# The last row of a down projection, multiplied in two parts of the tokens

## The chip, the cores and the metric

The kernel runs on one core of a Trainium2 chip. The metric is the device time of one execution in microseconds (us). A core has TensorE (PE in the rows; its weight loads are shown as PEld), VectorE (DVE), ScalarE (ACT), GpSimd (POOL) and the queues that issue transfers (SPq and ACTq are those of SyncE and ScalarE).

## What is computed

One layer of a hybrid decoder for 288 tokens (256 of a prompt and 8 x 4 new ones), model width 1024. The part that matters is the end, the feed-forward block:

```python
h = rmsnorm(x, n_mlp_pre)
f = jnp.square(jax.nn.relu(h @ w_up)) @ w_down      # 1024 -> 4096 -> 1024
x = x + rmsnorm(f, n_mlp_post)
```

The root mean square of `f` is taken over all 1024 features of a token, so no token's output can be finished before all features of that token are known.

## The kernel before

Activations lie transposed: features on the 128 partitions, tokens along the columns. `x` and `mg` are 128 x 8 x 288 (eight rows of 128 features). Weights come from memory in blocks of two sub-blocks of 128 x 1024; `split_w` (L163, L164) splits each into a high and a low part of the rounded type fp32r, on ScalarE and VectorE. `take(s)` hands out sub-block s and has the next one split ahead; the parts come from the pool `splp` with three buffers. A second pool, `spx`, with two buffers, is used earlier in the kernel.

`mm3` (L200 to L202) forms one product with three matmuls: high times high, high times low, low times high. Each is a matmul of 288 columns with a weight load of its own.

The down projection (L826 to L833) runs over eight rows `m` of 128 output features; each sums 32 products `kc` (four sub-blocks of eight), so 96 matmuls, in one PSUM tile `dn`. After a row, `post` (L720, L721) takes the square into `q_f` and the row times its gain into `mg` on ScalarE, and VectorE adds the square to `ssf`. The square of row 7 is not added there: it goes to the norm as a second summand.

Behind row 7 the tail is written in a fixed order (`manual_schedule`, L838): `rsqrt_rows` multiplies `ssf` and the last square with a matrix of 1/1024, which sums over partitions (L208, plain fp32, two passes for each matmul in the rows), then the reciprocal root on ScalarE (L212) and a correction in three VectorE steps (L216 to L218) give the scale `s3` of all 288 tokens. Meanwhile TensorE puts `x` for rows 0 to 4 into PSUM through an identity (L841). Then VectorE multiplies rows of `mg` by the scale (L844), TensorE adds them to the sums (L847), ScalarE copies these out (L848); rows 5 and 6 are added by VectorE (L850) and row 7 is scaled and added by GpSimd (L851, L852) from a copy of the scale (L842). Five transfers (L853, L854) bring the eight rows to `o_y`, four from SP's queue and the last, rows 3 and 4, from ScalarE's.

Of the kernel before, what the change touches and what calls it, by code (L numbers as in the profile page):

```python
# [10 lines left out]
F32 = mybir.dt.float32  # L11
# [5 lines left out]
P = 128  # L17
D = 1024
KC = D // P
# [4 lines left out]
NT = SEQ + ND  # L24
# [5 lines left out]
PAST = 1024  # L30
EPS = 1e-6


LAST = ((0, 1), (1, 3), (3, 5), (5, 7))
PE_SUM = 5

POOL_LO = (24, 25)
POOL_ML = (1,)
# [23 lines left out]
V_PRE, V_POST, V_MPRE, V_MPOST, V_ATT, V_CONV, V_TAP = 0, 8, 16, 24, 32, 36, 40  # L62
# [42 lines left out]


@with_exitstack
def layer(ctx, tc, xt, vec, cst, kt, vt, st, wts, o_y, o_k, o_v, o_cs):
    nc = tc.nc
    cp = ctx.enter_context(tc.tile_pool(name="cp", bufs=1))  # L110
    act = ctx.enter_context(tc.tile_pool(name="act", bufs=6))
    nrm = ctx.enter_context(tc.tile_pool(name="nrm", bufs=1))
    rawp = ctx.enter_context(tc.tile_pool(name="rawp", bufs=3))
    splp = ctx.enter_context(tc.tile_pool(name="splp", bufs=3))
    ec = ExitStack()
    cv = ec.enter_context(tc.tile_pool(name="cv", bufs=1))
    pg = ctx.enter_context(tc.tile_pool(name="pg", bufs=2, space=PSUM))
# [9 lines left out]
    x = cp.tile([P, KC, NT], F32, name="x")  # L127
    vv = cp.tile([P, V_END], F32, name="vv")
# [17 lines left out]
    m1024 = cp.tile([P, P], F32, name="m1024")  # L146
    nc.vector.memset(m1024, 1.0 / 1024)
    ident = cp.tile([P, P], F32, name="ident")
# [7 lines left out]
    def split_w(s, parts=1, pool=splp, eng=None):  # L156
        raw = blocks[s // 2][:, (s % 2) * 1024:(s % 2) * 1024 + 1024]
        hi = pool.tile([P, 1024], F32R, tag="hi", name=f"hi{s}")
        lo = pool.tile([P, 1024], F32R, tag="lo", name=f"lo{s}")
        n = 1024 // parts  # L160
        for i in range(parts):
            cs = slice(i * n, (i + 1) * n)
            a = nc.scalar.copy(hi[:, cs], raw[:, cs])  # L163
            b = (eng or nc.vector).tensor_sub(lo[:, cs], raw[:, cs], hi[:, cs].bitcast(F32))  # L164
        splits[s] = a.ins, b.ins
        return hi, lo
# [10 lines left out]
    ready = {}  # L177

    def ahead(s):
        if s < 96 and s not in ready:  # L180
            ready[s] = split_w(s, parts=4 if s in (1, 2) or 25 <= s <= 28 else 1, eng=nc.gpsimd if s in POOL_LO else None)

    def take(s, n=1):

        ahead(s)
        for i in range(1, n + 1):
            ahead(s + i)
        return ready.pop(s)
# [8 lines left out]
    def mm3(ps, w, j, xh, xl, start, stop):  # L197
        hi, lo = w
        a = hi[:, j * P:(j + 1) * P]
        nc.tensor.matmul(ps, lhsT=a, rhs=xh, start=start, stop=False)  # L200
        nc.tensor.matmul(ps, lhsT=a, rhs=xl, start=False, stop=False)  # L201
        return nc.tensor.matmul(ps, lhsT=lo[:, j * P:(j + 1) * P], rhs=xh, start=False, stop=stop)  # L202

    def rsqrt_rows(ssq, mean_w, n, dst, nm, pool=None, tag="g"):

        ps = (pool or pg).tile([P, 512], F32, tag=tag, name=f"ss_{nm}")
        for i, q in enumerate(ssq):
            nc.tensor.matmul(ps[:, :n], lhsT=mean_w, rhs=q, start=i == 0, stop=i == len(ssq) - 1)  # L208
        y = nrm.tile([P, NT], F32, tag="y", name=f"y_{nm}")
        t = nrm.tile([P, NT], F32, tag="t", name=f"t_{nm}")  # L210
        if nm == "f":
            e = nc.scalar.activation(y[:, :n], ps[:, :n], AF.Abs_reciprocal_sqrt, bias=epsc)  # L212
        else:
            nc.scalar.activation(y[:, :n], ps[:, :n], AF.Ln, bias=epsc)
            e = nc.scalar.activation(y[:, :n], y[:, :n], AF.Exp, scale=-0.5)
        nc.vector.scalar_tensor_tensor(t[:, :n], y[:, :n], -0.5, y[:, :n], ALU.mult, ALU.mult)  # L216
        nc.vector.scalar_tensor_tensor(t[:, :n], ps[:, :n], EPS, t[:, :n], ALU.add, ALU.mult)
        d = nc.vector.scalar_tensor_tensor(dst, t[:, :n], 1.5, y[:, :n], ALU.add, ALU.mult)  # L218
        return e.ins, d.ins

    def gemm(ps, w, bh, bl, between=()):

        for kc in range(KC):
            if 0 <= kc - 3 < len(between):
                between[kc - 3]()
            last = mm3(ps[:, :NT], w, kc, bh[kc // 4][:, kc % 4], bl[kc // 4][:, kc % 4], kc == 0, kc == KC - 1)
        return last.ins
# [43 lines left out]
    c = ap.tile([P, C_END], F32, name="c")  # L271
# [71 lines left out]
    with tc.manual_schedule(engines={mybir.EngineType.PE, mybir.EngineType.DVE, mybir.EngineType.Activation}):  # L343
# [4 lines left out]
        for kc in range(3):  # L348
            input_square(kc)
        ahead(4)  # L350
        for kc in range(3, 5):
            input_square(kc)
# [78 lines left out]
    def p_values(p):  # L431
        pts = []
        for j in range(2):
            s = soft.pop((p, j))
            tp = pa.tile([P, 512], F32, tag="a", name=f"tp{p}{j}")
            for i in range(3):
                nc.tensor.transpose(tp[:, i * P:(i + 1) * P], s[:, i * P:(i + 1) * P], ident)
            pt = sm.tile([P, 3 * P], F32, tag="pt", name=f"pt{p}{j}")
            nc.scalar.copy(pt, tp[:, 0:3 * P])
            pts.append(pt)  # L440
        return [lambda: p_sum(p, pts)]
# [188 lines left out]
    p = p_values(0)  # L630
    p_scores(1)
    conv_u(0, 13, p + [lambda: 0, lambda: d_transpose(0)])
    p = p_values(1)
# [6 lines left out]
    p = p_values(2)  # L640
# [6 lines left out]
    p = p_values(3)  # L647
# [21 lines left out]
    pt = ctx.enter_context(tc.tile_pool(name="pt", bufs=6, space=PSUM))  # L669
    spx = ctx.enter_context(tc.tile_pool(name="spx", bufs=2, side="right"))  # L670
# [17 lines left out]
    ws = [take(24, 0)]  # L688
# [20 lines left out]
    tp = ctx.enter_context(tc.tile_pool(name="tp", bufs=1))  # L709
    tw = ctx.enter_context(tc.tile_pool(name="tw", bufs=2))  # L710
    mg = tp.tile([P, KC, NT], F32, name="mg")
    fh = tp.tile([P, 32, NT], F32R, name="fh")
    fl = tp.tile([P, 32, NT], F32R, name="fl")

    def post(ps, m, vcol, dst, ssq, nm):

        t = ssq
        if m:
            t = tw.tile([P, NT], F32, tag="q", name=f"q_{nm}{m}")
        nc.scalar.square(t, ps[:, :NT])  # L720
        nc.scalar.mul(dst, ps[:, :NT], vv[:, vcol + m:vcol + m + 1])  # L721
        if 0 < m < 7:
            nc.vector.tensor_add(ssq, ssq, t)
        return t
# [7 lines left out]
    for m in range(8):  # L732
        if m < NW:
            mix_half(m, 1, False)
            ps = pss[m]
        else:
            w = take(24 + m, m < 7)
            ps = pt.tile([P, 512], F32, tag="o", name=f"mix{m}")
            gemm(ps, w, mh, ml)
        last = post(ps, m, V_POST, mg[:, m], ssm, "m")  # L740
# [4 lines left out]
    hl = [act.tile([P, 4, NT], F32R, tag="act", name=f"hl{i}") for i in range(2)]  # L745

    rsqrt_rows([ssm, last], m1024, NT, s1, "mix")
    warm(WARM1, "mix", last)
    ss1 = tp.tile([P, NT], F32, tag="ss1", name="ss1")
# [35 lines left out]
    ws = [take(32 + m, 0) for m in range(2)] + [split_w(34 + m, pool=spx) for m in range(2)]  # L785
# [25 lines left out]
    for m in range(NW, 32):  # L811
        w = take(32 + m)
        ps = (pg if m == 6 else pt).tile([P, 512], F32, tag="g" if m == 6 else "o", name=f"up{m}")
        last = gemm(ps, w, hh, hl)
# [8 lines left out]
    with tc.issue_after(evacuated):  # L823
        nc.scalar.preload_act_table_set("abs_reciprocal_sqrt_and_small")
    ssf = tp.tile([P, NT], F32, tag="ssm", name="ssf")
    for m in range(8):  # L826
        ps = pt.tile([P, 512], F32, tag="o", name=f"dn{m}")
        for j in range(4):
            w = take(64 + 4 * m + j)
            for k in range(8):  # L830
                kc = 8 * j + k
                mm3(ps[:, :NT], w, k, fh[:, kc], fl[:, kc], kc == 0, kc == 31)
        last = post(ps, m, V_MPOST, mg[:, m], ssf, "f")  # L833

    s3 = pg.tile([P, 512], F32, tag="g", name="s3")[:, :NT]
    s3c = nrm.tile([P, NT], F32, tag="s", name="s3c")
    sums = [pt.tile([P, 512], F32, tag="o", name=f"sum{m}") for m in range(PE_SUM)]
    with tc.manual_schedule(engines={mybir.EngineType.PE, mybir.EngineType.DVE, mybir.EngineType.Activation}):  # L838
        rsqrt_rows([ssf, last], m1024, NT, s3, "f")
        for m in range(PE_SUM):  # L840
            nc.tensor.matmul(sums[m][:, :NT], lhsT=ident, rhs=x[:, m], start=True, stop=False)  # L841
        nc.scalar.copy(s3c, s3)  # L842
        for a, b in LAST:
            nc.vector.tensor_mul(mg[:, a:b], mg[:, a:b], s3.unsqueeze(1).to_broadcast([P, b - a, NT]))  # L844
            if a < PE_SUM:
                for m in range(a, b):
                    nc.tensor.matmul(sums[m][:, :NT], lhsT=ident, rhs=mg[:, m], start=False, stop=True)  # L847
                    nc.scalar.copy(mg[:, m], sums[m][:, :NT])  # L848
            else:
                nc.vector.tensor_add(mg[:, a:b], mg[:, a:b], x[:, a:b])  # L850
    nc.gpsimd.tensor_mul(mg[:, 7], mg[:, 7], s3c)  # L851
    nc.gpsimd.tensor_add(mg[:, 7], mg[:, 7], x[:, 7])  # L852
    for e, a, b in ((nc.sync, 0, 1), (nc.sync, 7, 8), (nc.sync, 1, 3), (nc.sync, 5, 7), (nc.scalar, 3, 5)):  # L853
        e.dma_start(out=o_y[:, a:b], in_=mg[:, a:b])  # L854


# [61 lines left out]
```

## Time and profile before

| | us |
|---|---|
| time, median of 2 runs | 378.39 (378.39 to 378.40) |
| time of the profiled execution | 378.67 |
| its span | 376.9 |
| TensorE busy | 366.9 |
| VectorE busy | 226.6 |
| ScalarE busy | 198.6 |

The rows come from one profiled execution. A row gives engine, line, operation, and the tiles as output <- inputs. A matmul's duration reaches from its start to its modelled end; matmuls overlap, so the distance between starts and the duration differ.

### The profile page before, as it was taken

Reading aid. Unit: us, or ns where it says so; the run is one execution under the profiler, and the core shown is the slowest. Engines: PE = TensorE matmul, PEld = TensorE weight load, DVE = VectorE, ACT = ScalarE, POOL = GpSimd, SP = SyncE. Lnnn points to the kernel's source line nnn. Section 1 sums busy time; section 2 is a strip of 40 time slices with the busy share of each in tenths; the row PEclk is TensorE's granted clock in tenths of the full one; section 3 lists DMA queues with packets and bytes.
Section 4 is the critical chain, followed back from the end, with each engine's and each line's share of the span. In section 5 each row is a group of like instructions: output and inputs, shape, how many; then the busy total and the mean of one; then the engine's idle time right before and its main releaser. Section 6 shows DMA issues by size and latency. Waiting matters only on the chain.

```text
span 376.9 us, 6798 instructions
## 1 busy us (share of the span) xinstructions
PE 366.9 (97%) x2738; PEld 338.6 (90%) x2738; DVE 226.6 (60%) x414; ACT 198.6 (53%) x373; POOL 29.8 (8%) x56
## 2 busy tenths in 40 slices
PE   7999999999999999999999999999999999999994
PEld 6899688676885899899999999999999999999992
DVE  3889766457385877598886666666434344434404
ACT  4879546443463857446775555555533344434412
POOL 0006100114223300000000000000000000000001
PEclk9999999999999999999999999999999999999999
DMA  7995699986993426503435445453535263533003
GB/s 212 420 406 205 246 393 421 407 339 250 405 418 133 129 103 225 222 3 113 178 156 163 174 148 190 138 198 123 213 118 217 111 216 121 202 135 111 2 0 125
DMA packets 17647, 76.23 MB, mean 202 GB/s; under 512 B 2000, under 2 KB 7632, under 8 KB 10704
## 3 DMA queue, kind: packets, MB, share of 16 engines
q1 hardware_dynamic: 16464, 74.26, 52.8%
q10 hardware_dynamic: 1152, 1.54, 1.1%
q8 instruction: 21, 0.34, 0.3%
q14 instruction: 10, 0.08, 0.1%
HBM read 73.40 MB, written 2.40 MB: 201 GB/s over the span
## 4 chain that ended last, share of the span: by engine, by line
PE 86%; DVE 6%; ACT 2%; DMA 2%; issue 1%; SPq 1%; POOL 0%; DVEq 0%; ACTq 0%
PE dn L200 9%; PE dn L202 9%; PE dn L201 9%; PE up L200 8%; PE up L202 8%; PE up L201 8%; PE d L470 3%; PE dpv L514 2%; PE mix L202 2%; PE mix L200 2%; PE mix L201 2%; DMA raw<-wts 2%; PE qk L202 2%; PE qk L200 2%; PE qk L201 2%; PE u L200 1%
## 5 line engine op out<-in xcount | busy, mean ns | idle before, releaser
L164 DVE TENSOR_TENSOR lo<-raw,hi 128x1024 fp32r<-128x1024 f32 (+1 forms) x99 | 112.1, 1140 | 78.6 <-ACT hi L163 78.4
L163 ACT CAST hi<-raw 128x1024 fp32r<-128x1024 f32 (+1 forms) x104 | 97.5, 950 | 96.4 <-PE dn L201 55.3
L200 PE MATMUL dn<-fh,hi 128*128 128x288 f32 x256 | 75.8, 296 | 0.0
L201 PE MATMUL dn<-fl,hi 128*128 128x288 f32 x256 | 75.6, 295 | 0.0
L202 PE MATMUL dn<-fh,lo 128*128 128x288 f32 x256 | 75.3, 294 | 0.0
L201 PE MATMUL up<-hl,hi 128*128 128x288 f32 x248 | 73.4, 296 | 0.0
L200 PE MATMUL up<-hh,hi 128*128 128x288 f32 x248 | 73.1, 296 | 0.0
L202 PE MATMUL up<-hh,lo 128*128 128x288 f32 x248 | 72.9, 294 | 0.0
L202 PEld LDWEIGHTS dn<-fh,lo 128*128 128x128 f32 x256 | 48.2, 188 | 0.0
L201 PEld LDWEIGHTS dn<-fl,hi 128*128 128x128 f32 x256 | 48.0, 188 | 0.0
L200 PEld LDWEIGHTS dn<-fh,hi 128*128 128x128 f32 x256 | 48.0, 187 | 0.0
L202 PEld LDWEIGHTS up<-hh,lo 128*128 128x128 f32 x248 | 46.7, 188 | 0.1
L201 PEld LDWEIGHTS up<-hl,hi 128*128 128x128 f32 x248 | 46.6, 188 | 0.1
L200 PEld LDWEIGHTS up<-hh,hi 128*128 128x128 f32 x248 | 46.4, 187 | 0.0
L795 DVE SCALAR_TENSOR_TENSOR r<-up,s 128x288 f32<-128x288 f32 x32 | 14.2, 456 | 14.1 <-PE up L202 14.1
L200 PE MATMUL mix<-mh,hi 128*128 128x288 f32 x64 | 19.3, 302 | 0.0
L851 POOL TENSOR_TENSOR mg<-mg,s3c 128x288 f32<-128x288 f32 x1 | 0.8, 795 | 233.7 <-ACT s3c L842 233.7
L201 PE MATMUL mix<-ml,hi 128*128 128x288 f32 x64 | 19.0, 296 | 0.0
L202 PE MATMUL mix<-mh,lo 128*128 128x288 f32 x64 | 18.9, 295 | 0.0
L798 DVE TENSOR_TENSOR fl<-r,fh 128x288 fp32r<-128x288 f32 x32 | 14.0, 450 | 0.0
L797 ACT CAST fh<-r 128x288 fp32r<-128x288 f32 x32 | 13.3, 431 | 0.7
L796 ACT ACTIVATE r<-r 128x288 f32<-128x288 f32 x32 | 13.5, 438 | 0.0
(241 smaller groups left out, 637.6 us busy)
## 6 DMA issues: line engine op xcount, KB each, us to landing
raw<-wts SPq DMA_DIRECT2D x45, 1024.0 KB, 4.8
k<-kt SPq DMA_DIRECT2D x16, 640.0 KB, 11.7
v<-vt SPq DMA_DIRECT2D x9, 1024.0 KB, 11.7
raw<-wts SPq DMA_DIRECT2D x4, 512.0 KB, 8.5
v<-vt SPq DMA_DIRECT2D x2, 512.0 KB, 11.0
c<-cst SPq DMA_DIRECT2D x1, 838.0 KB, 9.7
raw<-wts SPq DMA_DIRECT2D x3, 256.0 KB, 5.3
x<-xt SPq DMA_DIRECT2D x4, 144.0 KB, 3.5
```

The source lines that it names most:

```text
L163: a = nc.scalar.copy(hi[:, cs], raw[:, cs])
L164: b = (eng or nc.vector).tensor_sub(lo[:, cs], raw[:, cs], hi[:, cs].bitcast(F32))
L200: nc.tensor.matmul(ps, lhsT=a, rhs=xh, start=start, stop=False)
L201: nc.tensor.matmul(ps, lhsT=a, rhs=xl, start=False, stop=False)
L202: return nc.tensor.matmul(ps, lhsT=lo[:, j * P:(j + 1) * P], rhs=xh, start=False, stop=stop)
L470: nc.tensor.matmul(ps[32 * i:32 * i + 32, 0:n], lhsT=qbd[:, p, 4 * g + i], rhs=t[:, i, 0:n], start=p == 0, stop=p == 3, tile_position=(0, ...
L514: nc.tensor.matmul(dpv[g][32 * i:32 * i + 32], lhsT=pt[:, j, 32 * i:32 * i + 32], rhs=t[i], start=False, stop=j == 4, tile_position=(0, 32 ...
L795: nc.vector.scalar_tensor_tensor(r, ps[:, :NT], 0.0, s2, ALU.max, ALU.mult)
L796: nc.scalar.square(r, r)
L797: a = nc.scalar.copy(fh[:, m], r)
L798: nc.vector.tensor_sub(fl[:, m], r, fh[:, m].bitcast(F32))
L851: nc.gpsimd.tensor_mul(mg[:, 7], mg[:, 7], s3c)
```

## The change

Row 7 leaves the loop. Its products are formed twice: first for tokens 0 to 159 (`last[0]`), then for tokens 160 to 287 (`last[1]`). Six of the 32 steps into the second part (18 matmuls) the norm of the first part is put into TensorE's order, and its scaling and addition run on VectorE. After the second part the same follows for its 128 tokens, with rows 0 to 3 added on TensorE in one matmul of 512 columns and rows 4 to 7 on VectorE. GpSimd no longer takes part. The sub-blocks 92 and 93 are split into the pool `spx`. The output is two tensors, one for each part, written by two transfers each.

```diff
-            ready[s] = split_w(s, parts=4 if s in (1, 2) or 25 <= s <= 28 else 1, eng=nc.gpsimd if s in POOL_LO else None)
+            ready[s] = split_w(s, pool=spx if s in (92, 93) else splp, parts=4 if s in (1, 2) or 25 <= s <= 28 else 1, eng=nc.gpsimd if s in POOL_LO else None)
...
             nc.tensor.matmul(ps[:, :n], lhsT=mean_w, rhs=q, start=i == 0, stop=i == len(ssq) - 1)
+            if mid and i == 0:
+                mid()
...
-    for m in range(8):
+    for m in range(7):
...
+    def last_row(i, kc):
+        if len(ws) <= kc // 8:
+            ws.append(take(92 + kc // 8))
+        c = cols[i]
+        mm3(last[i][:, :c.stop - c.start], ws[kc // 8], kc % 8, fh[:, kc, c], fl[:, kc, c], kc == 0, kc == 31)
...
+    def evac_last(i):
+        n = cols[i].stop - cols[i].start
+        nc.scalar.square(qs[i][:, :n], last[i][:, :n])
+        nc.scalar.mul(mg[:, 7, cols[i]], last[i][:, :n], vv[:, V_MPOST + 7:V_MPOST + 8])
+
+    def scaled(i, h):
+        n = cols[i].stop - cols[i].start
+        a = mg[:, 4 * h:4 * h + 4, cols[i]]
+        nc.vector.tensor_mul(a, a, sc[i][:, :n].unsqueeze(1).to_broadcast([P, 4, n]))
+        return a
+
+    def summed(i, h):
+        nc.vector.tensor_add(ys[i][h], mg[:, 4 * h:4 * h + 4, cols[i]], x[:, 4 * h:4 * h + 4, cols[i]])
+
+    def scales(i, mid=None):
+        n = cols[i].stop - cols[i].start
+        rsqrt_rows([ssf[:, cols[i]], qs[i][:, :n]], m1024, n, sc[i][:, :n], f"f{i}", mid=mid)
+
+    for kc in range(32):
+        last_row(0, kc)
+    evac_last(0)
...
+        for kc in range(6):
+            last_row(1, kc)
+        scales(0)
+        for kc in range(6, 32):
+            last_row(1, kc)
+        for h in range(2):
+            scaled(0, h)
+            summed(0, h)
+        evac_last(1)
+
+        scales(1, lambda: nc.tensor.matmul(xs, lhsT=ident, rhs=x[:, 0:4, cols[1]], start=True, stop=False))
+        nc.tensor.matmul(xs, lhsT=ident, rhs=scaled(1, 0), start=False, stop=True)
+        nc.scalar.copy(ys[1][0].rearrange("p a t -> p (a t)"), xs)
+        scaled(1, 1)
+        summed(1, 1)
+    for h in range(2):
+        nc.sync.dma_start(out=o_ya[:, h], in_=ys[0][h])
+    nc.sync.dma_start(out=o_yb[:, 1], in_=ys[1][1])
+    nc.scalar.dma_start(out=o_yb[:, 0], in_=ys[1][0])
```

## Rows read from the trace of the kernel before

**Rows 1.** The page, busy us, share of the span and instructions of an engine.
```profile
PE 366.9 (97%) x2738; PEld 338.6 (90%) x2738; DVE 226.6 (60%) x414; ACT 198.6 (53%) x373; POOL 29.8 (8%) x56
```
**Rows 2.** The page, chain that ended last, shares of the span by engine.
```profile
PE 86%; DVE 6%; ACT 2%; DMA 2%; issue 1%; SPq 1%; POOL 0%; DVEq 0%; ACTq 0%
```
**Rows 3.** Busy time by stretch: stretch, length, engines, granted clock, DMA share, GB/s.
```profile
165.00:352.00 187.00, 186.75 (x1400) 186.41 (x1399) 107.11 (x148) 95.16 (x148) 0.00 (x0) 1.00 0.43 153
352.00:365.40 13.40, 13.40 (x103) 13.40 (x102) 2.82 (x3) 2.80 (x4) 0.00 (x0) 1.00 0.00 1
365.40:376.90 11.50, 6.69 (x26) 4.12 (x24) 4.59 (x8) 3.69 (x9) 1.59 (x2) 0.98 0.28 103
```
**Rows 4.** Groups by line and shape, TensorE: busy us, mean ns, idle before.
```profile
L200 PE MATMUL dn<-fh,hi 128*128 128x288 f32 x256 | 75.8, 296 | 0.0
```
**Rows 5.** Order of time, 365.4 us to the end: start us, us, what.
```profile
365.40 0.65 PE L208 MATMUL ss_f<-ssf,m 128*128 128x288 f32 x2
365.60 0.41 ACT L720 ACTIVATE q_f<-dn 128x288 f32<-128x288 f32 x1 [8.68 <-PE dn L202]
...
366.06 0.75 PE L208 MATMUL ss_f<-q_f,m 128*128 128x288 f32 x2
...
366.65 2.59 PE L841 MATMUL sum<-x,ident 128*128 128x288 f32 x10
366.85 0.50 ACT L212 ACTIVATE y_f<-ss_f,epsc 128x288 f32<-128x288 f32 x1 [0.45 <-PE ss_f L208]
367.38 0.46 DVE L216 SCALAR_TENSOR_TENSOR t_f<-y_f 128x288 f32<-128x288 f32 x1 [9.21 <-ACT y_f L212]
...
368.37 0.47 DVE L218 SCALAR_TENSOR_TENSOR s<-t_f,y_f 128x288 f32<-128x288 f32 x1
...
369.30 2.45 DVE L844 TENSOR_TENSOR mg<-mg,s 128x288 f32<-128x288 f32 x4 [0.46 <-ACT s3c L842]
...
369.81 2.87 PE L847 MATMUL sum<-mg,ident 128*128 128x288 f32 x10 [0.57 <-DVE mg L844]
...
370.60 0.40 ACT L848 COPY mg<-sum 128x288 f32<-128x288 f32 x1 [1.33 <-PE sum L847]
...
371.78 0.76 DVE L850 TENSOR_TENSOR mg<-mg,x 128x576 f32<-128x576 f32 x1
373.14 0.34 ACTq L854 DMA_DIRECT2D o_y<-mg  x1
```
**Rows 6.** Order of time near 120 us: eight matmuls of 16 columns and their loads.
```profile
120.31 0.99 PEld L525 LDWEIGHTS dsel<-c,om 128*128 128x128 f32 x8
```
**Rows 7.** Order of time and group by shape: warm-up passes of 128 columns.
```profile
155.16 3.29 PE L243 MATMUL warm_mix<-q_m,m 128*128 128x128 f32 x28
...
L243 PE MATMUL warm_mix<-q_m,m 128*128 128x128 f32 x28 | 3.3, 275 | 0.0
```
**Rows 8.** Groups by line and shape, weight loads: busy us, mean ns, idle before.
```profile
L202 PEld LDWEIGHTS dn<-fh,lo 128*128 128x128 f32 x256 | 48.2, 188 | 0.0
...
L470 PEld LDWEIGHTS d<-k,qbd 128*32 128x32 f32 x128 | 3.6, 109 | 4.1 <-issue 1.7 <-POOL k L464 0.3
...
L525 PEld LDWEIGHTS dsel<-c,om 128*128 128x128 f32 x16 | 2.3, 190 | 0.0
```
**Rows 9.** Groups by line and shape, ScalarE: busy us, mean ns, idle before.
```profile
L497 ACT COPY dpt<-dt 128x512 f32<-128x512 f32 x2 | 1.2, 578 | 0.1
...
L214 ACT ACTIVATE y_attd<-ss_attd,epsc 128x32 f32<-128x32 f32 x1 | 0.3, 287 | 0.1
```
**Rows 10.** DMA issues from 340 us on: KB each, median us to landing.
```profile
o_y<-mg SPq DMA_DIRECT2D x2, 288.0 KB, 2.3
o_y<-mg SPq DMA_DIRECT2D x2, 144.0 KB, 1.8
o_y<-mg ACTq DMA_DIRECT2D x1, 288.0 KB, 2.7
```

## What the change was predicted to do

> **What bounds the kernel now.** The page comes first: TensorE is busy for 366.9 of 376.9 us [rows 1], and the chain that ended last runs over TensorE for 86% of the span [rows 2]. The next view is the table of stretches. Between 165 and 352 us, 1400 products take 187.00 us, 0.1336 us each, at the full granted clock (2.4 GHz), and TensorE does not pause. The last 11.5 us hold only 6.69 us of it [rows 3]. So two things set the time: the pitch of the products, and the tail behind the last one.
>
> The pitch first. A product has 288 columns and lasts 296 ns in the row by shape [rows 4], but the next starts after 0.134 us, so the pitch is the price, not the duration. Each product brings a 128x128 weight load of its own: the loads (338.6 us busy) number as many as the matmuls, 2738 [rows 1].
>
> The tail is read from the order of time [rows 5]. The last product's columns are through when the first matmul of ss_f starts at 365.40; I call this T0. The square starts at T0+0.20, ss_f's second pair at T0+0.66, the reciprocal root at T0+1.45, three VectorE steps of about 0.49 each from T0+1.98 on (the third at T0+2.97), the first multiplication at T0+3.90, and from there VectorE, TensorE and ScalarE hand pairs of rows on until the last output transfer is issued at 373.14, T0+7.74. The span ends 3.76 us later, at 376.9.
>
> **The change part by part.**
>
> *The products.* Row 7's 96 products of 288 columns become 96 of 160 and 96 of 128. The columns stay the same, 96 x 288, but the weight loads double: 96 more. What a product costs when its columns no longer cover its load is the term that decides, and no product of the split (fp32r) type with fewer than 288 columns is in the trace. Its neighbours are. In dsel eight matmuls of only 16 columns stand in a row: eight loads in 0.99 us, the last lasting 0.19, so (0.99 - 0.19)/7 = 0.114 us from load to load, though there is next to nothing to stream [rows 6]. In the warm-up, 28 passes of 128 columns take 3.29 us, one lasts 0.275: 3.01/27 = 0.112 us [rows 7]. A load's length grows from 109 ns (32 columns) to 188 (128) [rows 8]: 79 ns for 96 columns, 0.82 ns each, so 128 columns occupy the load path for at least 0.105 us; the rest of the 188 ns is latency that overlaps. Loads of the products' type and of the unsplit type last 188 and 190 ns [rows 8], so I take 0.112 us for each of the 192: 21.5 us in place of 96 x 0.1336 = 12.8. The products get **8.7 us dearer**. Lower bound: 0.105, +7.3 us. Upper bound: the pitch of 0.1336 does not fall at all, because it is already that of the loads and not of the columns: 96 x 0.1336 = +12.8 us.
>
> The Trainium skill (TensorE: Matmul & The Clock Gate, Back-to-back issue gap) gives about 81 ns for a pair of load and matmul at 128 columns; by it 192 would be 15.6 us, an estimate, and the products would get only 2.8 us dearer. The same page's section on LDWEIGHTS gives columns / 1.2, 107 ns for a load, which speaks against this change; the 0.112 to 0.114 us of this trace agree with the second.
>
> *The first part's end.* Square, scaling, ss_f0, root, two multiplications and two additions over 160 tokens run behind the second part. Its cover: after the insertion 26 x 3 products remain, 78 x 0.112 = 8.7 us, against under 6 us of chain: 1.45 + 0.53 + 3 x 0.5 to the scale at most [rows 5], then two pairs of VectorE passes over 640 elements, each about 0.76 + 64 x 1.04 ns = 0.83 us (288 elements take 0.46, 576 take 0.76: 1.04 ns for one [rows 5]), 3.3 us together: 6.8 at the very most. If the cover were gone, that would be added. The 18 products ahead of the insertion (2.0 us) cover the square and its latency of some 0.66. Only ss_f0's four passes of 160 columns stand on TensorE. A pass of 288 takes (2.59 - 0.17)/10 = 0.242 [rows 5] (0.17 is the latency that the 0.275 of a 128-column pass has beyond its pitch of 0.112 [rows 7]), one of 128 0.112, so 0.81 ns a column: 0.138 for 160, **+0.55 us**.
>
> *The weights.* Splits 92 and 93 move to the other pool, so all four stand while both parts use them. Row 7 lasted 12.8 us, and in the 13.40 us up to T0 ScalarE was busy for 2.80 and VectorE for 2.82, with no weight transfer left (1 GB/s) [rows 3]. A group of 24 products lasts 2.7 us now in place of 3.2, so the splits stay hidden; uncovered, one would cost TensorE at most the 2.8 us.
>
> *The tail,* by the same steps with 128 columns. ScalarE: 0.50 us against 0.287 for 288 and 32 columns [rows 5, 9], 0.83 ns a column, so each step loses 0.13; VectorE loses 160 x 1.04 = 0.17. From T0: ss_f1's first pair 0.22; the new product of the identity and four rows of x, 512 columns in two passes, 2 x (0.112 + 384 x 0.81 ns) = 0.85, to T0+1.07. The squares would be there at 0.53, so this product holds the second pair up by half a microsecond. Second pair 0.22, latency 0.17, wake-up 0.04: root at T0+1.50, against 1.45. Then 0.40, 0.32, 0.33 and 0.33: multiplication at T0+2.88, against 3.90. It has 512 elements, 0.69 us, to 3.57. TensorE adds: 0.79 us from matmul to copy for 288 columns [rows 5], and 2 x 224 x 0.81 ns more, 1.15, with the hand-over 4.75. The copy of 512 columns out of PSUM is 0.58 [rows 9], so the issue comes at T0+5.35: 2.4 us earlier. The other half (multiplication and addition, 1.4 us behind 3.57) is issued at about T0+5.0 from SP. The o_ya transfers are long out, so in place of five transfers of 1.18 MB two of 256 KB are left; landing takes 1.8 us for 144 KB and 2.3 to 2.7 for 288 KB [rows 10]. I take 0.25 off the last. **Tail: -2.65 us**; bounds -2.1 (nothing off the landing, 0.3 of hand-overs more) and -3.3 (landing in 1.8).
>
> *Sum.* 8.7 + 0.55 - 2.65 = +6.6. The profiled execution took 378.67 (span 376.9 and 1.8 around it), so it would take 385.3; the median shown is 378.39, 0.28 lower: **385.0 us**, 1.7% slower.
>
> **Rivals.**
>
> *The load's cost does not shrink (or a part under 256 columns streams at half rate).* For it: the pitch of 0.1336 is 11% over 288 columns at 2.4 GHz (0.120), and nothing shows what fills the rest; a pass of the unsplit type streams two cycles a column, and 160 and 128 columns would cost 0.138 + 0.112 = 0.250 against 0.267 for two full pitches. Against it: both types' loads last as long [rows 8]. Time: +11.2 to 12.8, so 387.5 to 389.6. From a pitch of about 0.117 on, the result is over 2% slower.
>
> *The columns set the pace and loads hide.* This is the case that is not slower, and it decides once the pitch is below 0.078 (12.8 + 2.65 - 0.55 over 192): 96 x 288 columns cost 12.8 us as before, and at most 96 fixed shares of 0.0136 (0.1336 - 0.120) come on top, 1.3 us. Then 0 to 1.3 + 0.55 - 2.65: 376.3 to 377.6 us. For it: the loads run beside the matmuls. Against it: dsel, whose loads had nothing to wait for but each other [rows 6]. By the Trainium skill's 81 ns (same page and section as above) it would come out near this case, at 379.1, an estimate; the 0.112 and 0.114 of this trace do not agree with it.
>
> *Narrow products fall back to the unsplit type's two double passes.* Then a pair of parts costs 2 x 0.138 + 2 x 0.112 = 0.50 us, 96 of them 48: +35.2, to 411.5 us. Against it: TensorE runs every product of the trace as one instruction; but none is narrower than 288.
>
> **How the numbers follow.** The forecast (pitch 0.105 to 0.117) gets 0.56, the costlier load 0.25, the columns 0.06, the fall-back 0.12, a gain over 2% 0.01. The predicted time is the likeliest one's, 385.0. The range joins the first two: low is 378.39 + 7.3 + 0.55 - 3.3, so 382.9; high is 378.39 + 12.8 + 0.55 - 2.1 = 389.6; together 0.81. About 2% (7.6 us) is what a measurement of this kernel can tell from no change; the forecast lies within it at 6.6. Faster by over 2%: 0.01; within: 0.56 + 0.06 = 0.62; slower: 0.25 + 0.12 = 0.37.
>
> **What would show it.** In the profile after: 192 products of row 7 in 21.5 us (pitch 0.112) and not 12.8, 25.6 or 48; no gap in TensorE between the parts; the root of the second part 1.5 us behind the last product, the last issue 5.35 us behind it; the first part's VectorE work ended before that. A pitch of 0.117 or more, or a pause at the insertion, makes the forecast wrong to the slow side; a pitch under 0.09 to the fast side.

## The result and the profile after

The changed kernel takes 385.33 us (median of 2 runs, 385.29 to 385.36) against 378.39 before: a ratio of 1.0176, 95% interval 1.0159 to 1.0193. That is 6.9 us slower, 1.8%, and within 2%. The forecast was 385.0 with a range of 382.9 to 389.6. The profiled execution took 385.36 with a span of 383.6, against 376.9.

The first view is the order of time at the places that set row 7's length (start us, us, engine, line, what): the first narrow product, the change from part one to part two, the inserted norm, and the last product.

```profile
352.83 0.24 PE L198 MATMUL dn<-fh,hi 128*128 128x160 f32 x1
...
363.52 0.26 PE L198 MATMUL dn<-fh,hi 128*128 128x128 f32 x1
...
365.51 0.49 PE L206 MATMUL ss_f<-ssf,m 128*128 128x160 f32 x2
365.84 0.43 PE L206 MATMUL ss_f<-q_f,m 128*128 128x160 f32 x2
366.00 0.33 PE L198 MATMUL dn<-fh,hi 128*128 128x128 f32 x1
366.17 0.27 PE L199 MATMUL dn<-fl,hi 128*128 128x128 f32 x1
...
374.66 0.27 PE L200 MATMUL dn<-fh,lo 128*128 128x128 f32 x1
374.77 0.43 PE L206 MATMUL ss_f<-ssf,m 128*128 128x128 f32 x2
```

Part one, 96 products of 160 columns, goes from 352.83 to 363.52: 10.69 us, 0.1114 each. The first 18 products of part two, with 128 columns, take 1.99 us, 0.1106 each. A fifth fewer columns, and the same pitch to within 1%: columns no longer set it. The inserted norm takes TensorE from 365.51 to 366.06, 0.55 us: the product behind it is recorded from 366.00 on, while it still waits, and the next one starts at 366.17, one pitch behind 366.06. The remaining 78 products run from 366.06 to 374.77, 8.71 us, 0.1117 each. Together 21.39 us of products in place of 12.8 [rows 3, 5].

The next view is the table of stretches (length, busy us of PE, PEld, DVE, ACT, POOL with instructions, granted clock, DMA share, GB/s). Nothing pauses on TensorE in row 7, its loads are busy all the time, and the clock stays at 1.00 (2.4 GHz). The 0.79 of the third stretch touches nothing here: in shorter stretches the clock is 1.00 up to 379.0 and 0.50 from 380.5 on, and TensorE's last operation ends at 379.57.

```profile
352.60:363.40 10.80, 10.80 (x98) 10.80 (x98) 0.46 (x1) 0.81 (x2) 0.00 (x0) 1.00 0.01 2
363.40:374.60 11.20, 11.20 (x102) 11.20 (x102) 4.18 (x7) 0.99 (x3) 0.00 (x0) 1.00 0.16 60
374.60:383.60 9.00, 2.81 (x11) 1.31 (x10) 2.86 (x6) 1.49 (x4) 0.00 (x0) 0.79 0.16 58
```

The end behind the last product, in order of time. T0 is now 374.77.

```profile
374.96 0.28 ACT L851 ACTIVATE q_f<-dn 128x128 f32<-128x128 f32 x1 [8.26 <-PE dn L200]
375.04 1.02 PE L882 MATMUL xs<-x,ident 128*128 128x512 f32 x2
...
376.32 0.37 ACT L212 ACTIVATE y_f<-ss_f,epsc 128x128 f32<-128x128 f32 x1 [0.82 <-PE ss_f L206]
...
377.70 1.29 DVE L857 TENSOR_TENSOR mg<-mg,s3b 128x512 f32<-128x512 f32 x2
...
379.61 0.59 ACT L884 COPY y<-xs 128x512 f32<-128x512 f32 x1 [2.92 <-PE xs L883]
...
380.22 0.34 ACTq L890 DMA_DIRECT2D o_yb<-y  x1
```

The root starts at T0+1.55 (1.45 before), the first multiplication at T0+2.93 (3.90), the last issue at T0+5.45 (7.74), and the span ends at T0+8.83 (11.5) [rows 3, 5]. The end is 2.67 us shorter.

The first part's work on VectorE lies behind the products. Its last pass ends 3.7 us ahead of T0:

```profile
366.74 0.33 DVE L216 SCALAR_TENSOR_TENSOR t_f<-y_f 128x160 f32<-128x160 f32 x1 [12.80 <-ACT y_f L212]
...
370.27 0.82 DVE L861 TENSOR_TENSOR y<-mg,x 128x640 f32<-128x640 f32 x1
```

The account against the span: products +8.57 (21.39 less 12.82), inserted norm +0.55, end -2.67, and 0.25 because row 7 began at 352.83 in place of 352.58 (T0 before less 96 pitches). No run explains this last term; in the runs below whose row 7 was read the row begins anywhere from 352.55 to 352.87. The sum, +6.70, is the difference of the spans, 6.7.

### The profile page after: what moved, and what is told of

It reads as the page before. It is cut to its first block, busy times and chain, and to the rows that moved or that the text cites. A ratio compares the mean times of both kernels' runs of the same rounds, so it can differ in the third digit from the quotient of the medians.

```text
span 383.6 us, 6960 instructions
## 1 busy us (share of the span) xinstructions
PE 372.1 (97%) x2822; PEld 344.7 (90%) x2822; DVE 229.0 (60%) x419; ACT 197.4 (51%) x371; POOL 28.3 (7%) x54
## 4 chain that ended last, share of the span: by engine, by line
PE 86%; DVE 6%; ACT 2%; DMA 2%; issue 1%; SPq 1%; POOL 0%; DVEq 0%; ACTq 0%
PE dn L198 10%; PE dn L200 10%; PE dn L199 10%; PE up L198 8%; PE up L200 7%; PE up L199 7%; PE d L470 3%; PE dpv L514 2%; PE mix L198 2%; PE mix L200 2%; PE mix L199 2%; DMA raw<-wts 2%; PE qk L200 2%; PE qk L198 2%; PE qk L199 2%; PE u L198 1%
## 5 line engine op out<-in xcount | busy, mean ns | idle before, releaser
L198 PE MATMUL dn<-fh,hi 128*128 128x288 f32 (+2 forms) x288 | 83.9, 291 | 0.0
L199 PE MATMUL dn<-fl,hi 128*128 128x288 f32 (+2 forms) x288 | 83.7, 291 | 0.0
L200 PE MATMUL dn<-fh,lo 128*128 128x288 f32 (+2 forms) x288 | 83.5, 290 | 0.0
L200 PEld LDWEIGHTS dn<-fh,lo 128*128 128x128 f32 x288 | 54.5, 189 | 0.0
L199 PEld LDWEIGHTS dn<-fl,hi 128*128 128x128 f32 x288 | 54.3, 189 | 0.0
L198 PEld LDWEIGHTS dn<-fh,hi 128*128 128x128 f32 x288 | 54.3, 188 | 0.0
L326 ACT COPY sw<-qk 32x288 f32<-32x288 f32 x32 | 12.5, 391 | 1.3 <-DVE qT L332 0.9
```

Source lines behind the costliest of these rows:

```text
L326: nc.scalar.copy(sws[i][32 * r:32 * r + 32], ps[32 * (r ^ 1):32 * (r ^ 1) + 32, :NT])
```

## The experiments

The question is whether the 8.6 us are the price of 96 more weight loads, or of columns streamed more slowly, of the new order, or of a fixed cost of any matmul. The kernel before was run on the same chip beside each group of experiments: its median was 378.91 us beside the first four, 378.61 beside the next four and 378.70 beside the last two. Ratios are to these.

**One part of the change alone: the products.** On the kernel before, row 7's products are split into columns 0 to 159 and 160 to 287 (`cols`), with sub-blocks 92 and 93 in `spx` as in the change, and the end stays whole.

```diff
...
+    for c in cols:
...
+        for kc in range(32):
...
+            mm3(ps[:, :n], ws[kc // 8], kc % 8, fh[:, kc, c], fl[:, kc, c], kc == 0, kc == 31)
+        nc.scalar.square(last[:, c], ps[:, :n])
...
```

> The kernel before with one part of the change alone: row 7's products in two parts (160 and 128 tokens), the end unsplit as before. If every product pays its own weight load (pitch 0.111 us each, as row 7 of the changed kernel shows), row 7 takes 192 x 0.1113 = 21.4 us in place of 12.8 and the time is 378.4 + 8.55 - 0.1 (a shorter last square) = 386.8 us, slower than the changed kernel by about 1.5, because the shorter end is missing. If instead the end's new order (the norm inserted among the products, other buffers) made the changed kernel slower and the split of the products were nearly free, the time stays within 1.3 us of 378.4 and the pitch of the narrow products lies below 0.08.

Measured: 387.29 us, ratio 1.0221 (1.0206 to 1.0237), +8.4 where +8.4 was expected. The products run from 352.72 to 374.11, 0.1114 us each, at the full clock, and the end is as long as before, 11.4 us (table of stretches):

```profile
352.70:374.00 21.30, 21.30 (x194) 21.30 (x192) 0.46 (x1) 1.40 (x4) 0.00 (x0) 1.00 0.01 2
374.00:385.50 11.50, 6.68 (x27) 4.28 (x26) 4.59 (x8) 3.44 (x9) 1.59 (x2) 1.00 0.28 103
```

So the split products alone cost more than the whole change does. The rest of the change is by the account above a gain of 2.1 us (2.67 - 0.55), which cannot pay for it; the two measured differences from the kernel before, +8.4 and +6.9, put this gain at 1.4, each with some 0.6 of uncertainty.

**Half the dose.** Sixteen of the 32 steps stay whole, sixteen are split.

```diff
...
+    for kc in range(16):
...
+        mm3(half[:, :NT], ws[kc // 8], kc % 8, fh[:, kc], fl[:, kc], kc == 0, kc == 15)
...
+    nc.scalar.copy(halfc, half[:, :NT])
+    for kc in range(16, 32):
+        last_row(0, kc)
+    nc.tensor.matmul(last[0][:, :TA], lhsT=ident, rhs=halfc[:, cols[0]], start=False, stop=True)
...
```

> The changed kernel with only half the dose: of row 7's 32 steps the first 16 are multiplied once with all 288 columns (their sum is copied out and added to each part by an identity product), the last 16 in two parts. Loads set the price: 48 extra loads in place of 96, 48 x (2 x 0.1113 - 0.1336) = +4.3, +0.5 for the four identity passes, +0.55 for the inserted norm, -2.65 for the end: 381.1 us; the end behind the last product stays at about 8.8 us, since ten steps (3.3 us) still cover most of the first part's work. If the cost came with the split as such (its inserted norm, the pool, the order) and not with each load, the time stays near 385.3. If the cover of 3.3 us is too short, the end grows by up to 1.5 us.

Measured: 381.41 us, ratio 1.0067 (1.0051 to 1.0084), +2.5 where +2.7 was expected. Row 7 with the norm and the identity passes takes 18.2 us in place of 12.8, the end 8.8:

```profile
352.50:370.70 18.20, 18.20 (x154) 18.20 (x153) 3.21 (x7) 2.19 (x6) 0.00 (x0) 1.00 0.01 2
370.70:379.50 8.80, 2.65 (x10) 1.15 (x9) 4.30 (x8) 1.49 (x4) 0.00 (x0) 0.79 0.35 134
```

Of the 5.4 us more in row 7 the inserted norm is 0.55 and the identity passes some 0.5 by the expectation's sum; the 4.3 that are left are half of 8.57. Half the extra loads cost half as much, and the end keeps its whole gain. Each step that is split costs 3 x (2 x 0.1113 - 0.1336) = 0.27 us of TensorE. So this shorter cover brings 2.7 us for 5.4. By these figures some six split steps would come out even ((2.7 - 1.05) / 0.27, with 1.05 for the norm and the identity passes, an estimate), if so short a cover still hides the first part's work; no run tried fewer than sixteen.

**Pitch against columns, measured by itself.** Series of 24 products of the split type between rows 6 and 7, nothing else changed.

```diff
+            for n in (16, 64, 128, 160, 192, 224, 256, 288, 320, 384, 512):
...
+                for i in range(24):
+                    nc.tensor.matmul(ser[:, :n], lhsT=w[0][:, (i % 8) * P:(i % 8 + 1) * P], rhs=flat[:, :n], start=True, stop=True)
```

> The kernel before with series of 24 products of the split type put between rows 6 and 7 of the down projection, their results unused: 16, 64, 128, 160, 192, 224, 256, 288, 320, 384 and 512 columns, each with a 128x128 weight load; then 64, 128 and 288 columns with weights of 32 columns; then 128 columns with the same weights each time. Load theory: pitch flat at 0.111 us up to some 240 to 260 columns, then growing with the columns (0.1336 at 288, about 0.227 at 512); with weights of 32 columns the pitch at 64 and 128 columns falls well below 0.1 us; with the same weights each time it stays at 0.111, since they are loaded again. If an instruction had a fixed floor of 0.111 whatever it loads, the narrow weights would change nothing. If columns under 256 streamed at half rate, 224 and 192 columns would take 0.19 and 0.16 us.

The pitch is the distance between the starts of two series, divided by 24 (order of time; this is one run, of 429.94 us with the series in it):

```profile
352.42 2.74 PE L839 MATMUL pitch16x<-fh,hi 128*128 128x16 f32 x24
355.01 4.41 PE L839 MATMUL pitch64x<-fh,hi 128*128 128x64 f32 x24
359.23 5.36 PE L839 MATMUL pitch128x<-fh,hi 128*128 128x128 f32 x24
364.39 5.35 PE L839 MATMUL pitch160x<-fh,hi 128*128 128x160 f32 x24
369.54 4.55 PE L839 MATMUL pitch192x<-fh,hi 128*128 128x192 f32 x24
373.93 2.86 PE L839 MATMUL pitch224x<-fh,hi 128*128 128x224 f32 x24
376.62 3.04 PE L839 MATMUL pitch256x<-fh,hi 128*128 128x256 f32 x24
379.50 3.32 PE L839 MATMUL pitch288x<-fh,hi 128*128 128x288 f32 x24
382.66 3.68 PE L839 MATMUL pitch320x<-fh,hi 128*128 128x320 f32 x24
386.18 4.33 PE L839 MATMUL pitch384x<-fh,hi 128*128 128x384 f32 x24
390.34 3.83 PE L839 MATMUL pitch512x<-fh,hi 128*128 128x512 f32 x16
```

At 16 columns 0.108 us, at 224 still 0.112; then 0.120 at 256, 0.132 at 288, 0.147 at 320, 0.173 from 384 to the next series. From 256 on this is the columns at 2.4 GHz plus 0.012 to 0.014 us, the same addition at each width; the floor and that line meet near 235 columns ((0.1113 - 0.0133) x 2.4 GHz, an estimate from these points). The next rows, one tile each, tell what the floor belongs to (duration min/median/max in ns, first and last start; PEld are the loads):

```profile
L843 PEld LDWEIGHTS narrow64x<-fh,hi x24: 108/110/114, 395.6 to 396.5; 128*32 128x32 f32 x24
L843 PE MATMUL narrow64x<-fh,hi x24: 192/195/201, 395.8 to 396.6; 128*32 128x64 f32 x24
...
L843 PE MATMUL narrow128x<-fh,hi x24: 221/223/227, 396.6 to 398.0; 128*32 128x128 f32 x24
...
L846 PEld LDWEIGHTS twice128x<-fh,hi x24: 187/192/192, 401.1 to 403.6; 128*128 128x128 f32 x24
L846 PE MATMUL twice128x<-fh,hi x24: 221/274/280, 401.2 to 403.7; 128*128 128x128 f32 x24
```

With weights of 32 columns the pitch falls to 0.035 us at 64 columns (0.8 / 23) and 0.061 at 128 (1.4 / 23). So a matmul as such has no floor of 0.11; one with 128 weight columns has. That it is the load and not the product is argued from two things: the pitch is nearly the same for 16 columns and for 224 (0.108 and 0.112), and with 32 weight columns the loads last 110 ns in place of 192. These products also have only 32 rows of output, so no run here parts the load from its product. With the same weights each time the pitch stays at 0.109 (2.5 / 23), and the trace has 24 loads: they are loaded again.

The values for 64 to 192 columns in this series are not those of the full clock, which is the miss of this run. The stretches show why:

```profile
352.00:354.50 2.50, 2.50 (x25) 2.50 (x23) 0.46 (x1) 0.80 (x2) 0.00 (x0) 1.00 0.03 7
354.50:359.00 4.50, 4.50 (x29) 4.50 (x30) 0.00 (x0) 0.00 (x0) 0.00 (x0) 0.67 0.00 0
359.00:364.50 5.50, 5.50 (x27) 5.50 (x28) 0.00 (x0) 0.00 (x0) 0.00 (x0) 0.50 0.00 0
```

One microsecond into the series of 64 columns, right behind that of 16, the granted clock fell to 0.50 (1.2 GHz): it is 1.00 from 355.5 to 356.0 and 0.51 in the next half microsecond. It came back at 373.1, near the end of the series of 192. At 0.50 the pitch at 128 and 160 columns is 0.215 us, twice the floor: the floor goes with TensorE's clock. At the full clock 128 and 160 columns are known from the changed kernel, 0.111.

**Other parts: 256 and 32.** As many products and loads, a shorter last part.

```diff
-TA = 160
+TA = 256
```

> The changed kernel with the parts 256 and 32 in place of 160 and 128: the same number of products and loads. If a load of 0.111 us bounds a narrow product, 96 products of 32 columns still take 10.7 us (pitch 0.111), those of 256 take 11.5 (columns: 256 at 2.4 GHz is 0.107, plus the 0.0136 that 288 columns show above theirs), 22.2 together; the inserted norm costs 0.87, and the end behind a part of 32 tokens is about 6.1 us in place of 8.8: 383.3 us. If columns set the pace, the products of 32 columns take 0.03 us each and the time falls to about 375. If narrow products stream at half rate, 32 columns are bound by the load and 256 by the full rate, and the time is the same as under the load theory; the pitch series tells these two apart.

Measured: 389.92 us, ratio 1.0293 (1.0278 to 1.0309), 6 us above the load theory's sum, and on no theory's number. The table of stretches shows a cause that was in none of them:

```profile
364.00:369.10 5.10, 5.10 (x45) 5.00 (x43) 1.49 (x4) 1.23 (x3) 0.00 (x0) 1.00 0.01 3
369.10:380.00 10.90, 10.90 (x53) 10.90 (x53) 4.59 (x4) 0.00 (x0) 0.00 (x0) 0.50 0.24 96
380.00:387.90 7.90, 3.50 (x15) 3.07 (x15) 1.36 (x6) 0.93 (x4) 0.00 (x0) 0.50 0.06 17
```

TensorE never paused, but from 369.1 us on, in the midst of products of 32 columns, the granted clock was 0.50. The 57 products that were left, from 369.07 to T0 at 381.23, took 0.213 us each in place of the 0.111 of the products of 32 columns before the fall, which is 5.8 us; the end behind them took 6.7 us in place of the 6.1 expected.

**The same with more columns in flight.** The second part multiplies tokens 160 to 287 and uses the last 32.

```diff
...
-        c = cols[i]
-        mm3(last[i][:, :c.stop - c.start],
+        c = (cols[0], slice(160, NT))[i]
+        mm3(wide[i][:, :c.stop - c.start],
```

> The parts 256 and 32 again, but the second part's products run over 128 columns, tokens 160 to 287, of which only the last 32 are used: as many products, loads and results as with 256 and 32, only more columns in flight. If the run with 32 columns was slow because the granted clock fell to half during its narrow products (0.50 from 369 us on), the clock stays at 1.00 here as it does with 128 columns in the changed kernel, and the sum holds that was made for 256 and 32: products 96 x 0.120 + 96 x 0.1113 = 22.2 us, the inserted norm 0.87, the end about 6.1 us: 383.3, against 378.4 before. If the end for 32 tokens or the larger first part was the cause, the time stays near 389.

Measured: 383.12 us, ratio 1.0117 (1.0102 to 1.0132), against 383.3 expected. The clock stays at 1.00 through both parts:

```profile
352.90:364.40 11.50, 11.50 (x99) 11.50 (x99) 0.46 (x1) 0.80 (x2) 0.00 (x0) 1.00 0.01 1
364.40:375.70 11.30, 11.30 (x101) 11.20 (x99) 6.08 (x7) 1.23 (x3) 0.00 (x0) 1.00 0.19 76
375.70:381.50 5.80, 1.42 (x11) 1.12 (x9) 1.36 (x6) 0.93 (x4) 0.00 (x0) 0.83 0.17 59
```

More arithmetic made it nearly 7 us faster, and the sum for 256 and 32 holds once the clock does. The fall of the clock is thereby shown as the cause of the loss, and the narrow second part as what brought the fall; VectorE's work and the transfers of the first part run beside the products here too. What it is in the narrow products that brings the clock down stays open. Of the versions that split every step this is the best, and still 4.5 us slower than the kernel before; with sixteen steps split it was 2.5.

**The x product behind the norm.** On the changed kernel.

```diff
-        scales(1, lambda: nc.tensor.matmul(xs, lhsT=ident, rhs=x[:, 0:4, cols[1]], start=True, stop=False))
+        scales(1)
+        nc.tensor.matmul(xs, lhsT=ident, rhs=x[:, 0:4, cols[1]], start=True, stop=False)
```

> The changed kernel with the product of the identity and four rows of x (512 columns, two passes) issued behind the second pair of the last norm and not between its pairs. If that product holds the second pair up, as the prediction's sum has it, the root of the second part starts about 0.5 us earlier, T0+1.05 in place of T0+1.55, and all behind it too: 0.5 us less than the changed kernel, 384.8 us against 385.3. If the root waits for the squares alone, nothing changes.

Measured: 384.48 us, ratio 1.0153 (1.0138 to 1.0169) against 1.0176 for the changed kernel. In its trace T0 is 374.46 and the root starts at 375.51, T0+1.05 in place of 1.55; the span ends 8.34 us behind T0 in place of 8.83. The half microsecond is as the sum had it.

```profile
375.51 0.37 ACT L212 ACTIVATE y_f<-ss_f,epsc 128x128 f32<-128x128 f32 x1 [0.32 <-PE ss_f L206]
```

**A better end for the kernel before.** Four attempts, with the products whole.

The scale in SBUF, without ScalarE's copy:

```diff
-    s3 = pg.tile([P, 512], F32, tag="g", name="s3")[:, :NT]
...
+    s3 = nrm.tile([P, NT], F32, tag="s", name="s3")
...
-        nc.scalar.copy(s3c, s3)
...
```

> The kernel before, its products left whole, with one change in the end: the scale is written to SBUF by the third VectorE step, so that ScalarE's copy of it for GpSimd falls away. In the kernel before the first multiplication starts 0.43 us after that copy began. If it waits for the copy, it now starts at T0+3.47 in place of 3.90 and the time falls by 0.4 us, 378.0 on the scale of 378.4; if not, it stays.

Measured: 379.26 us, ratio 1.0016 (1.0007 to 1.0026), a little slower. The first multiplication does start earlier, 3.46 us behind T0 (365.18), but the four take 3.66 us in place of 2.45 [rows 5]:

```profile
368.64 3.66 DVE L842 TENSOR_TENSOR mg<-mg,s 128x288 f32<-128x288 f32 x4
368.91 0.84 POOL L849 TENSOR_TENSOR mg<-mg,s 128x288 f32<-128x288 f32 x1 [233.44 <-DVE s L218]
```

The rows one by one show that only two of the three passes over 576 elements have grown, to 1.35 and 1.34 us. The third starts when GpSimd's two instructions are over and takes 0.74, as all three did before (745 ns, the last row, of the kernel before, by shape):

```profile
369.02 1.35 DVE L842 TENSOR_TENSOR mg<-mg,s 128x576 f32<-128x576 f32 x1
369.83 1.19 POOL L850 TENSOR_TENSOR mg<-mg,x 128x288 f32<-128x288 f32 x1
370.29 1.34 DVE L842 TENSOR_TENSOR mg<-mg,s 128x576 f32<-128x576 f32 x1
371.56 0.74 DVE L842 TENSOR_TENSOR mg<-mg,s 128x576 f32<-128x576 f32 x1
...
L844 DVE TENSOR_TENSOR mg<-mg,s 128x576 f32<-128x576 f32 x3 | 2.1, 745 | 0.0
```

The two slow passes end 0.62 and 0.61 us behind the ends of GpSimd's two instructions (369.75 and 371.02).

The scale in SBUF and the rows dealt out anew, two of them to GpSimd, with six transfers in place of five:

```diff
-LAST = ((0, 1), (1, 3), (3, 5), (5, 7))
+LAST = ((0, 1), (1, 3), (3, 4), (4, 6))
...
+    for r in (7, 6):
+        nc.gpsimd.tensor_mul(mg[:, r], mg[:, r], s3)
+        nc.gpsimd.tensor_add(mg[:, r], mg[:, r], x[:, r])
...
```

> The kernel before with whole products, the scale in SBUF and the end's rows dealt out anew: rows 0 to 3 added on TensorE and copied by ScalarE, rows 4 and 5 on VectorE, rows 6 and 7 on GpSimd. By the durations before (VectorE 0.46 to 0.76 a pass, ScalarE's copies 0.46 apart, GpSimd 0.8) the last issue comes at about T0+6.95 in place of 7.74: 0.8 us less than before, 377.6 on the scale of 378.4, and 0.4 less than with the scale in SBUF alone. If GpSimd's four passes slow VectorE's down or SP's queue of five issues becomes the last, the gain is that of the scale alone or none.

Measured: 380.35 us, ratio 1.0045 (1.0030 to 1.0060), 1.7 slower where 0.8 less was expected. More of GpSimd at the same time makes it worse: VectorE's four multiplications take 3.96 us for 1728 elements in place of 2.45 for 2016, and GpSimd's passes over 288 elements about 1.1 us (2.10 and 2.27 for two) in place of 0.8. VectorE's two passes over 576 elements, 1.34 and 1.35 us, again end 0.62 and 0.61 us behind the end of a GpSimd instruction.

The scale in SBUF and no GpSimd:

> As with the scale in SBUF, but GpSimd takes no part: VectorE scales and adds rows 5 to 7 itself, four output transfers in place of five. With the scale in SBUF and GpSimd at work VectorE's four multiplications took 3.66 us in place of 2.45. If it was GpSimd's work at the same time that slowed them, three of them (of 288 and 576 elements) return to about 0.46 and 0.66 us, the fourth and the addition (864 elements) take about 1.06 each, and the last issue comes at T0+7.5: 0.2 us less than before, about 378.1 on the scale of 378.4. If the operand in SBUF is slow by itself, the multiplications stay as long as with GpSimd and the time is about 379.5.

Measured: 378.92 us, ratio 1.0006 (0.9997 to 1.0015), no difference. VectorE's passes are back (groups by shape, busy us, mean ns):

```profile
L842 DVE TENSOR_TENSOR mg<-mg,s 128x576 f32<-128x576 f32 x2 | 1.4, 750 | 0.0
```

With the scale in SBUF the 576-element passes beside GpSimd took 1.34 to 1.35 us, without GpSimd 0.75: the two engines' simultaneous work on SBUF was the cause. The Trainium skill (SBUF — State Buffer, SBUF: two separate sides) says that a VectorE operation with two SBUF inputs and a GpSimd operation that reads SBUF exclude each other, for the whole instruction. The runs agree: each slow pass of 576 elements ends a fixed 0.61 to 0.62 us behind a GpSimd instruction, as one that had to wait for its end would, and with the scale in PSUM GpSimd did no harm (745 ns). The last issue comes at T0+7.3 here, yet the end is no shorter. The last two transfers, of 432 and 288 KB, land 3.1 and 3.3 us behind their issue, where the last of 288 KB took 2.7 before [rows 10]; that more rows are under way at once is a likely reason, not one that was tried.

The copy behind the first multiplication, the scale in PSUM:

```diff
...
-        nc.scalar.copy(s3c, s3)
         for a, b in LAST:
             nc.vector.tensor_mul(mg[:, a:b], mg[:, a:b], s3.unsqueeze(1).to_broadcast([P, b - a, NT]))
+            if a == 0:
+                nc.scalar.copy(s3c, s3)
...
```

> The kernel before, the scale left in PSUM, ScalarE's copy of it for GpSimd issued behind the first multiplication and not ahead of it. If the first multiplication waited for that copy, it starts at T0+3.47 in place of 3.90; GpSimd starts about 0.5 us later and still ends first. If nothing else waits for the copy, the last issue comes 0.4 us earlier (about 378.0 on the scale of 378.4); if the second multiplication now waits for it in the same way, the gain is lost there.

Measured: 378.67 us, ratio 1.0006 (0.9997 to 1.0015), no difference. The first multiplication starts at T0+3.47 (T0 is 365.78), as it would without the wait, and the wait moved to the second, as its row says:

```profile
369.25 0.45 DVE L843 TENSOR_TENSOR mg<-mg,s 128x288 f32<-128x288 f32 x1
...
370.17 2.08 DVE L843 TENSOR_TENSOR mg<-mg,s 128x576 f32<-128x576 f32 x3 [0.47 <-ACT s3c L845]
```

What makes one engine wait for the other, where both only read the scale, no run shows. No version tried here beats the kernel before.

## Why the prediction was right, step by step

**The products** were put at 0.112 us each and 8.7 us more; they took 0.1114 and 8.57 more. The step that carried this was the choice of row. The nearest row by name, a product of the same type, offered only its pitch of 0.1336, a bound; the rows that shared the limiting resource, dsel with 16 columns behind a full load [rows 6] and the warm-up with 128 [rows 7], gave the price to 3%. The pitch series bears the resource out: 0.108 to 0.112 us at 16 and at 224 columns, and far less with 32 weight columns.

**The costlier load or half-rate columns** (0.25) fell: 160 columns at half rate would have been 0.138 us, and they took 0.1114; nor did the pitch stay at 0.1336. The doubt behind it, what fills the 11% over 288 columns, is settled as far as it matters: it is a fixed 0.012 to 0.014 us for a product that is bound by its columns, and it does not come on top of the load. What it consists of stays open.

**The columns set the pace** (0.06) fell with the first part alone: 387.3 us against at most 379.7 by that theory. The 81 ns of the Trainium skill (TensorE: Matmul & The Clock Gate, Back-to-back issue gap) for a pair at 128 columns are not reached here, with 0.111. The section LDWEIGHTS (loading the stationary operand) of the same page of the Trainium skill puts a load at its columns / 1.2, in ns; by that 128 columns take 107, an estimate, within 4% of what was measured.

**The fall-back to two double passes** (0.12) fell: every narrow product is one instruction.

**The first part's end** was to be hidden by 8.7 us of products: 8.71 they were, and the work ended 5.6 us behind its insertion (the prediction has both "under 6 us" and 6.8 at the very most for it; the first was right, and either is covered). The inserted norm's 0.55 us came out at 0.55.

**The end**: predicted T0+1.50, 2.88, 4.75 and 5.35 for root, multiplication, copy and last issue; measured 1.55, 2.93, 4.84 and 5.45. The landing term (0.25 saved) came out at 0.4, and the sum, 2.65 predicted, 2.67 measured, is that close because the two small errors cancel: that is luck. In the same way the 0.25 us by which row 7 began later is in no term of the forecast, and the 0.13 that the products came out cheaper gave back half of it.

**What the prediction did not see** is that narrow products can cost the clock. It gave the fall of the clock no case of its own, and with 160 and 128 columns none occurred. With 32 columns the same sum would have missed by 6 us.

## What to carry to other kernels

The weights of a product that is cut along its columns are loaded once for each part: before cutting, find in the trace the shortest pitch of matmuls with hardly any columns behind a full load (0.11 us here), and charge every part at least that; by the pitch series, parts of 235 columns or more cost their columns and 0.013 us, and parts below all cost the same as long as the clock holds. What a cover hides (2.7 us of end here) has to be set against the whole price of making it (9.1 us), and with half the steps split the price fell to 5.4 us while the gain stayed, so try the smallest cover first. When narrow matmuls run back to back, look at the granted clock of that stretch as well, since a busy TensorE row does not show it.

## What the runs showed of the hardware that was not expected

The granted clock fell from 1.00 to 0.50 (2.4 to 1.2 GHz) while TensorE issued products without a pause: among products of 32 columns in one run, and among products of 64 columns right behind a series of 16 in another; it came back there during products of 192 columns. Through part two of the changed kernel, 96 products of 128 columns, it stayed at 1.00. At 1.2 GHz the pitch of the products of 32, 128 and 160 columns is 0.213 to 0.215 us, twice that at 2.4, so the floor follows the clock too.

VectorE's multiplications of 576 elements with both operands in SBUF took 0.74 to 0.75 us by themselves and 1.34 to 1.35 beside GpSimd, ending 0.61 to 0.62 us behind the end of a GpSimd instruction; with one operand in PSUM they took 0.745 beside GpSimd too.
